# A looped prefix-logsumexp kernel rebuilt in fp32: row sums inside partitions, two small matmuls, one broadcast join, four load and two store buffers

## The chip, the cores and the metric

The kernel runs on 1 core of one Trainium2 chip. The metric is the device time of one execution in microseconds (us); lower is better. A ratio is the one from the runs of two kernels in the same rounds; it is not quite the ratio of the medians quoted beside it. "Span" is the time that the profiler sees from the first to the last instruction, about 2 us less than the device time. In the profiles, ACT is ScalarE, DVE is VectorE, PE is TensorE (PEld its weight loads), POOL is GpSimd and SP is SyncE; PSUM is the memory into which the matmuls of these kernels write.

## The reference

```python
B, S, D = 8, 4096, 2048            # x: fp32, standard normal
out[:, 0] = x[:, 0]
for t in range(1, S):              # running log(sum(exp(x))) along S
    mx = maximum(out[:, t-1], x[:, t])
    out[:, t] = mx + log(exp(out[:, t-1] - mx) + exp(x[:, t] - mx))
```

So the output is log(cumsum(exp(x))) along S. It reads 268.4 MB and writes 268.4 MB.

## The kernel before

The input is cut into 64 tiles, 8 for each of the 8 batches. A tile is 128 partitions x 4 rows x 2048 columns in fp32, 4.19 MB, and is contiguous in memory: a partition holds four consecutive rows of S. Each tile goes through Exp (ACT), sums (PE and DVE) and Ln (ACT) in four column pieces of 512, in place, in one of five buffers.

```python
R, FD, NC, NB = 4, 512, 4, 5
io = [pool.tile([P, R, D], f32) for i in range(NB)]       # loaded, worked on and stored in place
et = [pool.tile([P, R, FD], bf16) for c in range(NC)]     # Exp of a piece
ps = [psum.tile([P, FD], f32) for c in range(NC)]

# SP: a load waits until its buffer has been stored
take(sp, stored[n], 16);  sp.dma_start(out=io[n][:], in_=x_v[...]).then_inc(loaded[n], 16)

# ACT, for each piece of a tile
act.activation(et[c][:], t[:, :, cols(c)], ACT.Exp)
act.activation(t[:, :, cols(c)], t[:, :, cols(c)], ACT.Ln)
# ... and one store of a whole tile: act.dma_start(out=dst, in_=io[n][:])

# PE, for each piece: 4 bf16 matmuls to the first rows' sums, 4 more to carry the piece's total on
for r in range(R): pe.matmul(ps[c][:], (Li if r == 0 else Ls)[:], et[c][:, r, :], ...)
for r in range(R): pe.matmul(ps[c][:], (Us if r == 0 else Ui)[:], et[c][:, r, :], ...)

# DVE, for each piece: one copy from PSUM and three adds of 512
dve.tensor_add(t[:, 1, sl], ps[c][:], et[c][:, 1, :])
dve.tensor_copy(t[:, 0, sl], ps[c][:])
dve.tensor_add(t[:, 2, sl], t[:, 1, sl], et[c][:, 2, :])
dve.tensor_add(t[:, 3, sl], t[:, 2, sl], et[c][:, 3, :])
# [cut: semaphores, loop bounds, the last tile's smaller stores]
```

The four masks Li, Ls, Ui and Us are built ahead of the block that holds the first load.

The softmax here doesn't subtract the row's maximum and nothing guards it: scores larger than these inputs give would overflow.

Of the kernel before, what the change touches and what calls it, by code (L numbers as in the profile page):

```python
# [9 lines left out]
def kernel(  # L10
# [19 lines left out]

    nc = tc.nc
    f32 = mybir.dt.float32
    bf16 = mybir.dt.bfloat16
# [9 lines left out]
    NC = D // FD  # L43
    NB = 5
    assert NC == 4 and NBLK >= 3

    const = ctx.enter_context(tc.tile_pool(name="const", bufs=1))
    Li = const.tile([P, P], bf16)
    masks.make_upper_triangular(nc, Li, val=1.0, diag=True)
    Ls = const.tile([P, P], bf16)  # L50
    masks.make_upper_triangular(nc, Ls, val=1.0, diag=False)
    Ui = const.tile([P, P], bf16)
    masks.make_lower_triangular(nc, Ui, val=1.0, diag=True)
    Us = const.tile([P, P], bf16)
    masks.make_lower_triangular(nc, Us, val=1.0, diag=False)
# [3 lines left out]
    io = [pool.tile([P, R, D], f32, name=f"io{i}", tag=f"io{i}") for i in range(NB)]  # L59
    et = [pool.tile([P, R, FD], bf16, name=f"et{c}", tag=f"et{c}") for c in range(NC)]  # L60
    ps = [psum.tile([P, FD], f32, name=f"ps{c}", tag=f"ps{c}") for c in range(NC)]

# [3 lines left out]
    def cols(c):  # L66
        return slice(c * FD, (c + 1) * FD)

    def take(engine, sem, n):

        engine.add_instruction(mybir.InstEventSemaphore(  # L71
            name=f"I-{nc.next_id()}", engine=engine.engine, ins=[], outs=[],
            sync_info=mybir.SyncInfo(
                on_wait=[mybir.SyncWait(
                    sync_type="semaphore", id=sem.num, ant_name=sem.name,
                    wait_mode="sem-ge-imm", wait_value=n,
                )],
                on_update=[mybir.SyncUpdate(
                    sync_type="semaphore", id=sem.num, ant_name=sem.name,
                    update_mode="sem-sub-imm", update_value=n,  # L80
                )],
            ),
        ))

    with tc.tile_critical():
        sem = lambda name: nc.alloc_semaphore(name)
        logs = sem("logs")
        parts = {c: sem(f"part{c}") for c in range(2, NC)}

        loaded = [sem(f"loaded{n}") for n in range(NB)]  # L90
        stored = [sem(f"stored{n}") for n in range(NB)]
        exps = [sem("exps0"), sem("exps1")]
        prefix = [sem("prefix0"), sem("prefix1")]
        copied = [sem("copied0"), sem("copied1")]
        added = [sem("added0"), sem("added1")]
        chain = [sem("chain0"), sem("chain1")]
        freed = [sem("freed0"), sem("freed1")]

        with nc.Block() as block:

            @block.sync
            def _(sp):
                def load(src, n):
                    sp.dma_start(out=io[n][:], in_=src).then_inc(loaded[n], 16)

                for i in range(NB):
                    load(x_v[i], i)
                turns = (NT - NB) // NB
                with sp.Fori(0, turns) as j:
                    for n in range(NB):  # L110
                        take(sp, stored[n], 16)
                        load(x_v[bass.ds(j * NB + (NB + n), 1)][0], n)
                for i in range(NB + turns * NB, NT):
                    take(sp, stored[i % NB], 16)
                    load(x_v[i], i % NB)
                for i in range(NT - NB, NT):

                    take(sp, stored[i % NB], 48 if i == NT - 1 else 16)

            @block.scalar  # L120
            def _(act):
                def exp(n, c):
                    t = io[n]
                    if c == 0:
                        take(act, loaded[n], 16)
                    act.activation(  # L126
                        et[c][:], t[:, :, cols(c)], ACT.Exp
                    )._wait_ge(freed[c % 2], c // 2 + 1).then_inc(exps[c % 2], 1)
                    if c >= 2:
                        take(act, freed[c % 2], 2)  # L130

                def ln(t, c, told=logs):
                    act.activation(  # L133
                        t[:, :, cols(c)], t[:, :, cols(c)], ACT.Ln
                    )._wait_ge(added[c % 2], c // 2 + 1).then_inc(told, 1)
                    if c >= 2:
                        take(act, added[c % 2], 2)

                def store(dst, n):
                    take(act, logs, NC)  # L140
                    act.dma_start(out=dst, in_=io[n][:]).then_inc(stored[n], 16)

                def turn(n, dst_above):
                    exp(n, 0)
                    if dst_above is not None:
                        ln(io[(n - 1) % NB], 2)
                    exp(n, 1)
                    if dst_above is not None:
                        ln(io[(n - 1) % NB], 3)
                        store(dst_above, (n - 1) % NB)  # L150
                    exp(n, 2)
                    ln(io[n], 0)
                    exp(n, 3)
                    ln(io[n], 1)

                turn(0, None)
                turns = (NT - 1) // NB
                with act.Fori(0, turns) as j:
                    for n in range(1, NB + 1):
                        turn(n % NB, o_v[bass.ds(j * NB + (n - 1), 1)][0])  # L160
                for i in range(1 + turns * NB, NT):
                    turn(i % NB, o_v[i - 1])
                last = stored[(NT - 1) % NB]
                t = io[(NT - 1) % NB]
                take(act, logs, 2)
                act.dma_start(
                    out=o_v[NT - 1][:, :, 0:2 * FD], in_=t[:, :, 0:2 * FD]
                ).then_inc(last, 16)
                for c in range(2, NC):
                    ln(t, c, parts[c])  # L170
                    take(act, parts[c], 1)
                    act.dma_start(  # L172
                        out=o_v[NT - 1][:, :, cols(c)], in_=t[:, :, cols(c)]
                    ).then_inc(last, 16)
                take(act, freed[0], 2)
                take(act, freed[1], 2)

            @block.tensor
            def _(pe):
                def front(c, first):  # L180
                    for r in range(R):
                        m = pe.matmul(  # L182
                            ps[c][:], (Li if r == 0 else Ls)[:], et[c][:, r, :],
                            start=first and r == 0, stop=r == R - 1, skip_group_check=True,
                        )
                        if r == 0:
                            m._wait_ge(exps[c % 2], c // 2 + 1)
                    m.then_inc(prefix[c % 2], 1)
                    if c >= 2:
                        take(pe, exps[c % 2], 2)  # L190

                def total(c, final):

                    if final:
                        pe.wait_ge(copied[c % 2], [1, 2, 2, 1][c]).then_inc(freed[c % 2], 1)
                    else:
                        for r in range(R):
                            m = pe.matmul(  # L198
                                ps[c][:], (Us if r == 0 else Ui)[:], et[c][:, r, :],
                                start=False, stop=r == R - 1, skip_group_check=True,  # L200
                            )
                            if r == 0:
                                m._wait_ge(copied[c % 2], [1, 2, 2, 1][c])
                        m.then_inc(freed[c % 2], 1)
                    if c in (1, 2):
                        take(pe, copied[c % 2], 2)

                def turn(first, final):
                    for c in range(NC):
                        front(c, first)  # L210
                        total((c - 1) % NC, first if c == 0 else final)


                pe.sem_inc(freed[0], 2)
                pe.sem_inc(freed[1], 1)
                with pe.Fori(0, B):
                    turn(True, False)
                    with pe.Fori(0, NBLK - 2):
                        turn(False, False)
                    turn(False, True)  # L220
                pe.wait_ge(copied[1], 1).then_inc(freed[1], 1)
# [60 lines left out]
```

## Time and profile before

| | before |
|---|---|
| device time, median | 1258.5 us (1257.97 to 1258.94, 4 runs) |
| span of the profiled run | 1256.5 us |
| busy: ACT, DVE, PE | 75%, 53%, 48% |
| DMA traffic, rate in the middle of the run | 536.9 MB, 433 GB/s |

First the page of the kernel before: busy time of each engine, then two rows of the 40 slices of the span (31.4 us each), namely the busy share of the DMA engines in tenths and what they moved.

```profile
## 1 busy us (share of the span) xinstructions
PE 605.2 (48%) x1872; PEld 196.9 (16%) x1920; DVE 659.9 (53%) x1024; ACT 936.7 (75%) x513; POOL 1.9 (0%) x12
...
DMA  8999999999999999999999999999999999999996
GB/s 377 423 433 432 433 433 433 433 432 434 432 431 432 434 434 433 434 433 434 433 434 434 434 433 432 434 434 433 432 433 433 434 431 434 432 432 431 434 434 275
```

No engine is near full, and the DMA row is 9 in all but the first and the last slice. This is the reading that everything else rests on: a tile is loaded and stored once, 8.39 MB, and at 433 GB/s that takes 19.4 us; 64 tiles take 1240 us of the 1256.5. The Trainium skill, "DMA: Bandwidth & Descriptors" (section "Issuing engines are not separate DMA queues"), says that DMAs of all issuing engines run on the same 16 DMA engines; the trace agrees: the queue of the loads and the queue of the stores each take 49.6% of those engines' time.

The groups of ACT in the kernel before; the columns are line, engine, operation, shapes and count, then busy us and mean ns of one, then idle time just ahead of them and who ended it:

```profile
L126 ACT ACTIVATE et<-io 128x2048 bf16<-128x2048 f32 x256 | 486.5, 1901 | 302.1 <-ACTq L71 283.6
L133 ACT ACTIVATE io<-io 128x2048 f32<-128x2048 f32 x256 | 484.8, 1894 | 2.5 <-DVE io L236 1.7
```

ACT idles ahead of Exp, and its own queue ends that idle time. ACTq L71 is the helper through which ACT waits for a semaphore, here mostly "the load has landed".

Last the ends of the run. In the stretches view of the kernel before, each line is one stretch of time: its length, busy us of PE, PEld, DVE, ACT and POOL (with instructions), the granted PE clock, the DMA share and GB/s.

```profile
0.00:40.00 40.00, 14.85 (x51) 5.00 (x52) 16.87 (x27) 24.33 (x14) 1.87 (x12) 0.97 0.92 380
40.00:80.00 40.00, 24.85 (x86) 8.63 (x88) 27.06 (x43) 38.39 (x22) 0.00 (x0) 0.86 1.00 432
80.00:1176.00 1096.00, 536.27 (x1648) 173.94 (x1688) 581.75 (x903) 823.94 (x452) 0.00 (x0) 0.79 1.00 433
1176.00:1200.00 24.00, 11.14 (x39) 3.84 (x40) 13.61 (x22) 17.02 (x10) 0.00 (x0) 0.86 1.00 431
1200.00:1230.00 30.00, 15.17 (x43) 4.75 (x44) 13.68 (x22) 22.39 (x13) 0.00 (x0) 0.77 0.85 366
1230.00:1256.00 26.00, 2.92 (x8) 0.74 (x8) 6.95 (x11) 10.66 (x6) 0.00 (x0) 0.55 0.80 325
```

Over 1096 us in the middle the DMA share is 1.00 at 433 GB/s. All that is not DMA at full rate lies in the first 40 and the last 56 us.

### The profile page before, as it was taken

Reading aid. Unit: us, or ns where it says so; the run is one execution under the profiler, and the core shown is the slowest. Engines: PE = TensorE matmul, PEld = TensorE weight load, DVE = VectorE, ACT = ScalarE, POOL = GpSimd, SP = SyncE. Lnnn points to the kernel's source line nnn. Section 1 sums busy time; section 2 is a strip of 40 time slices with the busy share of each in tenths; the row PEclk is TensorE's granted clock in tenths of the full one; section 3 lists DMA queues with packets and bytes.
Section 4 is the critical chain, followed back from the end, with each engine's and each line's share of the span. In section 5 each row is a group of like instructions: output and inputs, shape, how many; then the busy total and the mean of one; then the engine's idle time right before and its main releaser. Section 6 shows DMA issues by size and latency. Waiting matters only on the chain. (4 is left out here: it accounts for less than half of the span.)

```text
span 1256.5 us, 6996 instructions
## 1 busy us (share of the span) xinstructions
PE 605.2 (48%) x1872; PEld 196.9 (16%) x1920; DVE 659.9 (53%) x1024; ACT 936.7 (75%) x513; POOL 1.9 (0%) x12
## 2 busy tenths in 40 slices
PE   3555445454454444554445444455455444544542
PEld 1111111111111111111111111111111111111110
DVE  3656455464554544555546455464555544545443
ACT  5988778777787777877878778777787777877774
POOL 0000000000000000000000000000000000000000
PEclk9888687885888858878688786887857888578785
DMA  8999999999999999999999999999999999999996
GB/s 377 423 433 432 433 433 433 433 432 434 432 431 432 434 434 433 434 433 434 433 434 434 434 433 432 434 434 433 432 433 433 434 431 434 432 432 431 434 434 275
DMA packets 19875, 536.90 MB, mean 427 GB/s; under 512 B 2080, under 2 KB 2080, under 8 KB 3616
## 3 DMA queue, kind: packets, MB, share of 16 engines
q10 hardware_dynamic: 10656, 268.44, 49.6%
q1 hardware_dynamic: 9216, 268.44, 49.6%
q14 instruction: 3, 0.02, 0.0%
HBM read 268.44 MB, written 268.44 MB: 427 GB/s over the span
## 5 line engine op out<-in xcount | busy, mean ns | idle before, releaser
L126 ACT ACTIVATE et<-io 128x2048 bf16<-128x2048 f32 x256 | 486.5, 1901 | 302.1 <-ACTq L71 283.6
L133 ACT ACTIVATE io<-io 128x2048 f32<-128x2048 f32 x256 | 484.8, 1894 | 2.5 <-DVE io L236 1.7
L229 DVE TENSOR_TENSOR io<-ps,et 128x512 f32<-128x512 f32 x256 | 177.1, 692 | 570.9 <-PE ps L182 568.7
L182 PE MATMUL ps<-et,Li 128*128 128x512 bf16 x256 | 126.5, 494 | 628.6 <-ACT et L126 627.8
L182 PE MATMUL ps<-et,Ls 128*128 128x512 bf16 x768 | 280.9, 487 | 0.0
L198 PE MATMUL ps<-et,Ui 128*128 128x512 bf16 x624 | 213.0, 455 | 2.9 <-issue 0.4
L236 DVE TENSOR_TENSOR io<-io,et 128x512 f32<-128x512 f32 x256 | 177.1, 692 | 8.9
L233 DVE TENSOR_TENSOR io<-io,et 128x512 f32<-128x512 f32 x256 | 174.5, 681 | 0.0
L232 DVE COPY io<-ps 128x512 f32<-128x512 f32 x256 | 174.3, 681 | 0.0
L182 PEld LDWEIGHTS ps<-et,Li 128*128 128x128 bf16 x256 | 25.5, 100 | 787.4 <-ACT et L126 787.2
L182 PEld LDWEIGHTS ps<-et,Ls 128*128 128x128 bf16 x768 | 89.8, 117 | 98.1 <-issue 66.3
L198 PE MATMUL ps<-et,Us 128*128 128x512 bf16 x224 | 103.7, 463 | 0.3 <-DVE io L232 0.3
L198 PEld LDWEIGHTS ps<-et,Ui 128*128 128x128 bf16 x672 | 77.1, 115 | 113.4 <-issue 60.1
L198 PEld LDWEIGHTS ps<-et,Us 128*128 128x128 bf16 x224 | 26.1, 116 | 40.4 <-issue 22.7
L35 ACT ACT_TABLE_LOAD x1 | 1.3, 1283 | 0.8 <-PEq L266 0.8
masks.py:102 POOL TENSOR_SCALAR_AFFINE_SELECT Ui<-Ui 128x128 bf16<-128x128 bf16 x1 | 0.3, 296 | 0.0
masks.py:102 POOL TENSOR_SCALAR_AFFINE_SELECT Us<-Us 128x128 bf16<-128x128 bf16 x1 | 0.3, 295 | 0.0
masks.py:66 POOL TENSOR_SCALAR_AFFINE_SELECT Ls<-Ls 128x128 bf16<-128x128 bf16 x1 | 0.3, 294 | 0.0
masks.py:66 POOL TENSOR_SCALAR_AFFINE_SELECT Li<-Li 128x128 bf16<-128x128 bf16 x1 | 0.3, 293 | 0.0
masks.py:101 POOL MEMSET Ui<- 128x128 bf16 x1 | 0.2, 207 | 0.0
masks.py:101 POOL MEMSET Us<- 128x128 bf16 x1 | 0.2, 207 | 0.0
masks.py:65 POOL MEMSET Ls<- 128x128 bf16 x1 | 0.2, 206 | 0.0
(5 smaller groups left out, 0.6 us busy)
## 6 DMA issues: line engine op xcount, KB each, us to landing
io<-in_x_dram SPq DMA_DIRECT2D x64, 4096.0 KB, 31.5
out_dram<-io ACTq DMA_DIRECT2D x63, 4096.0 KB, 38.7
out_dram<-io ACTq DMA_DIRECT2D x1, 2048.0 KB, 11.1
out_dram<-io ACTq DMA_DIRECT2D x2, 1024.0 KB, 11.8
```

What stands on the lines that cost most here:

```text
L35: nc.scalar.preload_act_table_set("natural_log_exp_and_others")
L126: act.activation(et[c][:], t[:, :, cols(c)], ACT.Exp)._wait_ge(freed[c % 2], c // 2 + 1).then_inc(exps[c % 2], 1)
L133: act.activation(t[:, :, cols(c)], t[:, :, cols(c)], ACT.Ln)._wait_ge(added[c % 2], c // 2 + 1).then_inc(told, 1)
L182: m = pe.matmul(ps[c][:], (Li if r == 0 else Ls)[:], et[c][:, r, :], start=first and r == 0, stop=r == R - 1, skip_group_check=True,)
L198: m = pe.matmul(ps[c][:], (Us if r == 0 else Ui)[:], et[c][:, r, :], start=False, stop=r == R - 1, skip_group_check=True,)
L229: dve.tensor_add(t[:, 1, sl], ps[c][:], et[c][:, 1, :])._wait_ge(prefix[q], c // 2 + 1).then_inc(chain[q], 1)
L232: dve.tensor_copy(t[:, 0, sl], ps[c][:]).then_inc(copied[q], 1)
L233: dve.tensor_add(t[:, 2, sl], t[:, 1, sl], et[c][:, 2, :])._wait_ge(chain[q], base + 1).then_inc(chain[q], 1)
L236: dve.tensor_add(t[:, 3, sl], t[:, 2, sl], et[c][:, 3, :])._wait_ge(chain[q], base + 2).then_inc(added[q], 1)
```

## The change

The new kernel does the sums in fp32 and mostly on DVE. In each partition, three adds turn the four rows into running sums. One fp32 "triangle" matmul on the last row gives each partition the sum of all partitions ahead of it; one "carry" matmul with a mask that selects the last partition brings the total of all earlier tiles into the next tile's PSUM. One add then joins that PSUM row, broadcast over the four rows, to the tile. All steps work on half tiles of 1024 columns. Inputs have four buffers, freed by Ln and no longer by the store; outputs have two of their own. The masks are built by POOL beside the first loads.

```diff
-    NB = 5
+    NI, NO = 4, 2
+    HALF = D // 2
-    # [cut: four bf16 masks, built ahead of the block]
+    before = pool.tile([P, P], f32); last = pool.tile([P, P], f32)
-    io = [... for i in range(NB)]; et = [...bf16...]; ps = [psum.tile([P, FD], f32) ... 4]
+    ti = [pool.tile([P, R, D], f32) for i in range(NI)]
+    to = [pool.tile([P, R, D], f32) for i in range(NO)]
+    ps = [psum.tile([P, D], f32) for i in range(2)]
 # SP
-    take(sp, stored[n], 16); load(...)
+    sp.wait_ge(freed, n + 1); load(...)
 # ACT, a turn
-    exp 0, ln 2 (tile above), exp 1, ln 3 (tile above), store, exp 2, ln 0, exp 3, ln 1
+    exp(n, 0); exp(n, 1)
+    ln(n - 1, 0); ln(n - 1, 1)        # ln(.., 0) first takes stored[n % NO]
+    done(n - 1)                       # frees the input buffer
+    store(n - 1)
 # PE
-    8 bf16 matmuls for each of 4 pieces
+    triangle(k, h): 2 fp32 matmuls  ps[k % 2]       += before^T @ ti[k][:, 3, half h]
+    carry(k, h):    2 fp32 matmuls  ps[(k + 1) % 2]  = last^T   @ ti[k][:, 3, half h]
 # DVE
-    for each of 4 pieces: add, copy, add, add of 512
+    local(n, h): for r in 1..3: t[:, r, half] += t[:, r - 1, half]        # 3 adds of 1024
+    join(n, h):  t[:, :, half] += ps[n % 2][:, half] broadcast over r     # 1 add of 4096
```

(Semaphore bookkeeping and the last tiles' smaller stores are left out. In the last turn alone, Ln of tile 62's first half and its store stand ahead of Exp of tile 63.)

## The prediction

> **What bounds it now.** The DMA. The page's slices show the 16 DMA engines 90% busy or more and 431 to 434 GB/s in 36 of 40 slices; the DMA queue table gives 536.9 MB, half loads, half stores. 536.9 MB at 433.5 GB/s is 1238.5 us of the 1256.5 us span. The other 18 us are the ends: the stretch table shows the first 5 us at 105 GB/s, the 10 us stretches from 1216 us on at 383, 275, 403 and 184 GB/s. Per 4.19 MB tile that is 19.4 us of DMA, for load and store. ACT is busy 75% (14.6 us a tile), DVE 53%, PE 48%. The waits view agrees: Exp waits 284 us for its load (named ACTq), matmuls wait 627 us for Exp.
>
> **What the change does.** Same bytes, same 4 MB transfers. So it can only win at the ends, and lose if something else needs more than 19.4 us a tile.
>
> - ACT: 8 instructions of 2048 elements (1.80 us start to start) become 4 of 4096, about 3.5 us each: 14.2 us a tile. Slightly less.
> - DVE: 16 instructions of 0.60 to 0.71 us spacing (10.3 us a tile) become 6 dependent adds of 1024 and 2 joins of 4096 elements. The Trainium skill, "VectorE: DVE Perf Modes" (the TRN2 errata section), gives an fp32 add as (N+151)/0.96 ns; the trace agrees at 512 (692 ns). Estimate: 1.24 and 4.42 us, so 16.3 us a tile; DVE becomes the busiest engine, near 83 to 85%.
> - PE: about 29 bf16 matmuls a tile become 8 in fp32 (4 in a batch's last tile). "FP8 and Floating Point Precision" (TensorE Precision Notes) says true fp32 takes 4 passes; no trace here shows it yet. From the 0.42 us spacing at the low clock: 1.7 us each, 3.4 us a half, 14 us a tile cold, half of that warm.
> - The loop through DVE, by hand: local h0, local h1 (7.5 us), with triangle h0 behind local h1; join h0 with triangle h1 behind it; join h1 with carry h0; carry h1 under the next tile's local h0. Everything on PE hides if a half's two matmuls take under about 3.75 us; the loop is then 16.5 to 17 us. It reaches 19.4 us only if they take about 5 us.
> - Buffers: an input buffer is now held about 27 us from Exp's start to Ln's end rather than through the store, so 4 leave over 40 us for a load within 77 us. Two store buffers allow a store about 31 us; sharing DMA evenly with a load it needs 20 to 22. A load is always queued, so DMA should stay saturated.
> - Ends: loads no longer wait for four masks (about 1.8 us saved). The tail is coarser: half-tile Exp, adds, join, Ln, and 2 MB last stores; Exp of the last tile to the last store's landing about 33 us against about 32 before. Short moments with loads alone (419 GB/s in the stretch table) may cost some us.
>
> **Prediction: 1259 us, 1250 to 1273.** Faster by over 2%: 1%. Within 2%: 92%. Slower by over 2%: 7%.
>
> **Signs.** Right: DMA 9 in nearly all slices at about 433 GB/s; DVE near 84%, ACT near 73%; joins 4.4 us; fp32 matmuls 0.9 to 1.8 us; Exp or Ln waiting for DMA, not for PE. Wrong: DMA below 9 in the middle, Ln waiting for PE, DVE waiting for the triangle.
>
> **What would make it wrong.** Fp32 matmuls (with their weight loads) over 2.5 us; joins slowed by the PSUM broadcast to over 5.5 us; two store buffers making Ln wait so long that all load buffers fill and the queues run dry; a tail where tiles queue behind the 16.5 us loop without loads to fill DMA.

## The result, and the profile after

| | before | after |
|---|---|---|
| device time, median | 1258.5 us | 1259.14 us (1258.89 to 1259.56, 4 runs) |
| ratio | | 1.0006, 95% interval 0.9988 to 1.0023 |
| span | 1256.5 us | 1257.2 us |
| busy: ACT, DVE, PE | 75%, 53%, 48% | 73%, 81%, 52% |
| instructions | 6996 | 3678 |

The page of the changed kernel, the same rows as above:

```profile
PE 651.9 (52%) x960; PEld 215.2 (17%) x960; DVE 1023.2 (81%) x512; ACT 913.3 (73%) x257; POOL 1.1 (0%) x8
...
DMA  9999999999999999999999999999999999999997
GB/s 400 407 434 433 434 434 432 434 434 434 434 432 433 433 433 434 433 433 433 434 434 432 433 434 434 434 433 433 434 432 434 434 434 434 433 434 433 433 399 285
```

DVE's work rose by more than half, from 659.9 to 1023.2 us, and the middle of the GB/s row did not move. The groups of ACT, DVE and PE, from the same page:

```profile
L132 ACT ACTIVATE to<-ti 128x4096 f32<-128x4096 f32 x128 | 456.3, 3609 | 267.0 <-ACTq L61 258.5
L232 DVE TENSOR_TENSOR ti<-ti 128x1024 f32<-128x1024 f32 x384 | 464.7, 1224 | 211.3 <-ACT ti L127 202.6
L241 DVE TENSOR_TENSOR ti<-ti,ps 128x4096 f32<-128x4096 f32 x128 | 560.0, 4417 | 9.7 <-PE ps L208 9.0
L208 PE MATMUL ps<-ti,before 128*128 128x512 f32 x512 | 383.0, 900 | 352.6 <-DVE ti L232 352.2
L127 ACT ACTIVATE ti<-ti 128x4096 f32<-128x4096 f32 x128 | 455.9, 3609 | 66.9 <-ACTq L61 66.9
```

Read the third column. The joins (L241) wait 9 us in the whole run for PE, so PE hides. DVE's adds (L232) wait 203 us for Exp: DVE has time left. And Ln (L132) waits 258 us on a semaphore of ACT's queue, while Exp (L127) waits only 67. In the kernel before it was Exp that waited. Which semaphore Ln waits for shows in the time line of one tile in the changed kernel (start, length, what; the idle time ahead of it in brackets; PE's weight loads are left out):

```profile
616.91 0.35 ACTq L140 DMA_DIRECT2D out_dram<-to  x1
617.40 7.12 ACT L127 ACTIVATE ti<-ti 128x4096 f32<-128x4096 f32 x2 [0.72 <-ACTq L61]
621.05 7.40 DVE L232 TENSOR_TENSOR ti<-ti 128x1024 f32<-128x1024 f32 x6 [3.06 <-ACT ti L127]
624.85 3.42 PE L208 MATMUL ps<-ti,before 128*128 128x512 f32 x4 [13.00 <-DVE ti L232]
628.36 8.74 DVE L241 TENSOR_TENSOR ti<-ti,ps 128x4096 f32<-128x4096 f32 x2
628.50 1.98 PE L208 MATMUL ps<-ti,before 128*128 128x512 f32 x4 [0.24 <-DVE ti L232]
629.00 7.12 ACT L132 ACTIVATE to<-ti 128x4096 f32<-128x4096 f32 x2 [4.48 <-ACTq L61]
636.36 0.35 ACTq L140 DMA_DIRECT2D out_dram<-to  x1
```

Exp starts as soon as the store before it is issued (0.72 us, ACT's own issue). Then ACT is idle for 4.48 us ahead of the first of the two Ln. The signal from PE that this Ln also waits for follows the joins of its own tile, and these had ended at 617.98 us (609.23 + 8.75; the tile is the last of its batch and has no carry). What is left is the store buffer. The two stores of this window lie 19.45 us apart, which is the DMA's time for one tile. The landing times, from the parts "DMA issues" of the two pages, say the same. Before:

```profile
io<-in_x_dram SPq DMA_DIRECT2D x64, 4096.0 KB, 31.5
out_dram<-io ACTq DMA_DIRECT2D x63, 4096.0 KB, 38.7
```

After:

```profile
ti<-in_x_dram SPq DMA_DIRECT2D x64, 4096.0 KB, 28.8
out_dram<-to ACTq DMA_DIRECT2D x62, 4096.0 KB, 31.4
```

The last number is the median us from issue to landing. A store now lands in 31.4 us; with the 7.4 us of Ln and its issue that makes 38.8 us, two periods of 19.4, for two buffers. The store takes just as long as the loop allows it to.

The stretches of the changed kernel, beside which those of before can be laid:

```profile
0.00:40.00 40.00, 13.67 (x20) 4.53 (x20) 22.75 (x14) 22.77 (x7) 1.09 (x8) 0.92 0.96 406
40.00:80.00 40.00, 22.65 (x41) 7.29 (x40) 39.51 (x19) 35.23 (x10) 0.00 (x0) 0.93 0.99 413
80.00:1176.00 1096.00, 583.67 (x852) 192.98 (x852) 906.89 (x456) 800.64 (x226) 0.00 (x0) 0.77 1.00 433
1176.00:1200.00 24.00, 12.70 (x19) 4.59 (x20) 20.18 (x10) 18.80 (x6) 0.00 (x0) 0.81 1.00 433
1200.00:1230.00 30.00, 13.52 (x22) 3.90 (x20) 19.92 (x11) 23.76 (x8) 0.00 (x0) 0.78 0.89 381
1230.00:1256.00 26.00, 5.64 (x8) 1.85 (x8) 13.98 (x7) 12.15 (x4) 0.00 (x0) 0.63 0.73 290
```

The middle is equal: share 1.00, 433 GB/s. The ends can be turned into time by (difference in GB/s) x (length) / 433. In the first 40 us the change gains 2.4 us (406 against 380; the first load goes out at 1.03 us and not at 2.82). In the next 40 it loses 1.8 us: the first store is issued at 40.07 us against 34.72, when the four first loads have nearly drained (read from the trace, not tested by itself). From 1200 to 1230 it gains 1.0 us, and in the last 26 us it loses 2.1. The sum is a loss of about half a microsecond; the spans differ by 0.7.

### The profile page after: what moved, and what is told of

It reads as the page before. It is cut to its first block, busy times and chain, and to the rows that moved or that the text cites. A ratio compares the mean times of both kernels' runs of the same rounds, so it can differ in the third digit from the quotient of the medians. Undisturbed runs are those within 1.5% of the kernel's fastest.

```text
span 1257.2 us, 3678 instructions
## 1 busy us (share of the span) xinstructions
PE 651.9 (52%) x960; PEld 215.2 (17%) x960; DVE 1023.2 (81%) x512; ACT 913.3 (73%) x257; POOL 1.1 (0%) x8
## 5 line engine op out<-in xcount | busy, mean ns | idle before, releaser
L132 ACT ACTIVATE to<-ti 128x4096 f32<-128x4096 f32 x128 | 456.3, 3609 | 267.0 <-ACTq L61 258.5
L232 DVE TENSOR_TENSOR ti<-ti 128x1024 f32<-128x1024 f32 x384 | 464.7, 1224 | 211.3 <-ACT ti L127 202.6
L241 DVE TENSOR_TENSOR ti<-ti,ps 128x4096 f32<-128x4096 f32 x128 | 560.0, 4417 | 9.7 <-PE ps L208 9.0
L208 PE MATMUL ps<-ti,before 128*128 128x512 f32 x512 | 383.0, 900 | 352.6 <-DVE ti L232 352.2
L127 ACT ACTIVATE ti<-ti 128x4096 f32<-128x4096 f32 x128 | 455.9, 3609 | 66.9 <-ACTq L61 66.9
L197 PE MATMUL ps<-ti,last 128*128 128x512 f32 x448 | 268.9, 731 | 232.9 <-DVE ti L241 232.9
L208 PEld LDWEIGHTS ps<-ti,before 128*128 128x128 f32 x512 | 129.7, 281 | 621.4 <-DVE ti L232 513.4
L197 PEld LDWEIGHTS ps<-ti,last 128*128 128x128 f32 x448 | 85.4, 211 | 399.9 <-DVE ti L241 334.8
## 6 DMA issues: line engine op xcount, KB each, us to landing
ti<-in_x_dram SPq DMA_DIRECT2D x64, 4096.0 KB, 28.8
out_dram<-to ACTq DMA_DIRECT2D x62, 4096.0 KB, 31.4
```

The source lines that it names most:

```text
L127: act.activation(t[:, :, half(h)], t[:, :, half(h)], ACT.Exp).then_inc(exps[h], 1)
L132: act.activation(to[n % NO][:, :, half(h)], ti[n % NI][:, :, half(h)], ACT.Ln)._wait_ge(carried[h], turn + 1).then_inc(logs, 1)
L197: m = pe.matmul(ps[(k + 1) % 2][:, sl], last[:], ti[k % NI][:, R - 1, sl], start=True, stop=False, skip_group_check=True,)
L208: m = pe.matmul(ps[k % 2][:, sl], before[:], ti[k % NI][:, R - 1, sl], start=k == 0, stop=True, skip_group_check=True,)
L232: a = dve.tensor_add(t[:, r, half(h)], t[:, r - 1, half(h)], t[:, r, half(h)])
L241: dve.tensor_add(t[:, :, half(h)], t[:, :, half(h)], ps[n % 2][:, half(h)].unsqueeze(1).to_broadcast([P, R, HALF]),)._wait_ge(ahead[h], n ...
```

## The experiments

The theory: the DMA engines set the time of both kernels, at 19.4 us a tile; the new engine work fits under it; only the ends can differ. Rivals: (1) the changed kernel is paced by its own loop on the engines, and its 19.4 us a tile is a coincidence; (2) it is paced by the latency of its two store buffers, for which Ln visibly waits; (3) it lies on the edge, so that any added work would show. Each run below was taken in the same rounds and on the same chip as the kernel before, not always on one chip with its neighbours here. The changed kernel itself was not run again, so a difference to its 1259.14 us is one across chips; the median of the kernel before was 1258.27 to 1258.5 us on all of them.

### copy_only: the transfers without the compute

```diff
-    Exp, sums, Ln in between
+    act.wait_ge(loaded[i % 5], ...)
+    act.dma_start(out=o_v[i], in_=io[i % 5][:])     # 64 loads, 64 stores, nothing else
```

> Wrong result on purpose: only the same 64 loads and 64 stores of 4 MB, no compute, five buffers. If the DMA engines set the time of both kernels, 536.9 MB at about 433 GB/s is 1238.5 us, and with the start and the last landing 1243 to 1250 us. If the loop through the engines or through the two store buffers sets the 19.4 us a tile, the bare copy should be clearly faster, under 1200 us.

Measured: 1247.44 us (2 runs; wrong result), the kernel before 1258.36 on that chip. In the stretches view of this run, where the one engine listed is POOL:

```profile
80.00:1176.00 1096.00, 0.00 (x0) 1.00 1.00 433
```

With no compute at all the middle also moves 433 GB/s. Rivals 1 and 2 cannot be what sets that rate. All that either kernel could still win with these transfers is the 11 to 12 us between it and this copy, and these lie at the ends.

### a_quarter_store and b_quarter_store: what the DMA hides

```diff
-    act.dma_start(out=dst, in_=t)
+    act.dma_start(out=dst[:, 0:1, :], in_=t[:, 0:1, :])      # a quarter of the bytes, in both kernels
```

> The changed kernel with stores of a quarter of the bytes (wrong result on purpose); the DMA work falls from 19.4 to about 12.1 us a tile. If DMA bounds the changed kernel, it now falls to its loop through DVE, 16.4 to 17 us a tile: 1085 to 1130 us. If its compute is what takes 19.4 us a tile, it stays near 1255 us.

> The kernel before with stores of a quarter of the bytes (wrong result on purpose). If DMA bounds it, it falls to ACT's 14.6 us a tile: 960 to 1010 us, well below the changed kernel with the same cut, which would show the DVE work that the change adds and that the full stores hide. If it is bound by something else, it stays near 1255 us.

Measured: the changed kernel 1061.65 us, the kernel before 993.03 us (2 runs each, wrong results). Both fall once the DMA has less to do, so both were bound by their transfers; smaller stores also free the store buffers sooner (in 15.0 us), so this run alone does not tell the DMA's rate from rival 2. Below the DMA they are not equal: the changed kernel is 68.6 us slower, about 1.1 us a tile. This is the cost of the change that the full stores hide.

The expectation for the kernel before, 960 to 1010 us, held; that for the changed kernel, 1085 to 1130 us, missed by a little. Its time line shows the true length of the loop:

```profile
611.62 7.39 DVE L232 TENSOR_TENSOR ti<-ti 128x1024 f32<-128x1024 f32 x6
...
618.93 8.74 DVE L241 TENSOR_TENSOR ti<-ti,ps 128x4096 f32<-128x4096 f32 x2
...
627.59 7.39 DVE L232 TENSOR_TENSOR ti<-ti 128x1024 f32<-128x1024 f32 x6
```

From one tile's adds to the next tile's adds it takes 627.59 - 611.62 = 15.97 us, with DVE never idle in this tile, and not the predicted 16.5 to 17. The slack under the DMA is 19.4 - 16.0 = 3.4 us a tile.

### a_dve_plus4 and a_dve_plus2: filling the slack

```diff
+                def extra(i):                            # 1024 elements, into a tile that nobody reads
+                    m = last[:].unsqueeze(1).to_broadcast([P, 8, P])
+                    dve.tensor_add(spare[:], m, m)._wait_ge(spent, i).then_inc(spent, 1)
                         for h in range(2):
                             local(n, h)
+                            extra(...)                   # once: two a tile; twice: four a tile
                         # [cut: the spare tile, its semaphore, one wait for the masks]
```

> The changed kernel with four more adds of 1024 elements a tile on DVE, 4.9 us. If the hidden loop takes about 16.4 us, it is now about 21.3 us a tile and past the DMA's 19.4: 1390 to 1430 us, with DMA no longer full. If DVE has more slack than the loop says, it stays at 1259 us; if DVE were already the bound, it would rise by all 4.9 us a tile to 1570 us.

> The changed kernel with two more adds of 1024 elements a tile on DVE, 2.45 us, so the loop is about 18.8 us, still under the DMA's 19.4. If DMA bounds it: 1259 to 1266 us, the few us from the first and last tiles alone, DVE busy over 90%. If DVE's loop is the bound: plus 157 us, 1415 us.

Measured: four extra adds 1368.18 us (2 runs, ratio 1.087 to the kernel before), with joins 20.75 us apart in its time line (817.84 and 838.59); two extra adds 1263.43 us (4 runs, ratio 1.0038, interval 1.0022 to 1.0055). Both results are correct. With two, the middle is untouched although DVE is now 92% busy in the whole run; the stretch of that run:

```profile
80.00:1176.00 1096.00, 626.07 (x860) 195.65 (x860) 1038.11 (x573) 807.80 (x227) 0.00 (x0) 0.73 1.00 433
```

The 157 us of added DVE work cost about 4 us over the changed kernel, at the ends. With four, the loop passes 19.4 us, the time follows it, and the DMA is no longer at its rate:

```profile
80.00:1280.00 1200.00, 656.54 (x870) 211.22 (x869) 1188.12 (x696) 829.08 (x232) 0.00 (x0) 0.71 0.98 404
```

The expected 1390 to 1430 us was too high because it started from the 16.4 us loop; (20.75 - 15.97) / 4 gives 1.195 us for each added add. Rivals 1 and 3 fall: 2.4 us of added work a tile (two adds) cost nothing in the middle, 4.8 us (four adds) cost time; the edge at 3.4 us lies between.

### a_carry_x2: twice the carry work on PE

```diff
-                    for c in range(2 * h, 2 * h + 2):
+                    for c in [2 * h, 2 * h + 1] * 2:     # the second pair overwrites the first
```

> The changed kernel with each carry matmul done twice (same result, the second overwrites). At the warm clock a half's carry is then about 4 us and still hides: 1259 to 1265 us. At the cold clock it is 6.8 us, the loop 21.5 us, and the time near 1400 us. Between these it shows how often the clock is low. If PE were on the critical path already, it would rise in any case.

Measured: 1260.29 us (2 runs, correct, ratio 1.0012, interval 0.9992 to 1.0032), PE busy 61% in place of 52%. The stretch of that run:

```profile
80.00:1176.00 1096.00, 689.32 (x1250) 250.49 (x1248) 904.78 (x456) 802.66 (x226) 0.00 (x0) 0.86 1.00 433
```

The granted clock was 0.86 there against 0.77. PE has room. What a carry of twice the length would do at the low clock stays open, since the added work came with a higher clock.

### a_one_store_buf: one store buffer in place of two

```diff
-    NI, NO = 4, 2
+    NI, NO = 4, 1      # [cut: the last tiles' waits count both half stores]
```

> The changed kernel with one store buffer in place of two. Ln then waits for the whole store of the tile before: 7.4 us of Ln plus a store that shares DMA with the load for part of its time, about 14 us: 21.5 us a tile, 1330 to 1480 us, DMA no longer full. If two store buffers are already what paces the changed kernel by latency and not by the DMA's rate, one should double the tile to about 39 us, 2400 us.

Measured: 1915.46 us (2 runs, correct), ratio 1.52. Neither number was right: 30 us a tile, where the theory had 21.5 and rival 2 had 39. The time line of this run shows why:

```profile
815.43 7.12 ACT L132 ACTIVATE to<-ti 128x4096 f32<-128x4096 f32 x2 [15.13 <-ACTq L61]
822.77 30.35 SPq L111 DMA_DIRECT2D ti<-in_x_dram  x2
822.80 0.35 ACTq L140 DMA_DIRECT2D out_dram<-to  x1
...
845.45 7.12 ACT L132 ACTIVATE to<-ti 128x4096 f32<-128x4096 f32 x2 [15.05 <-ACTq L61]
```

The end of Ln frees an input buffer and an output buffer at once, so the next load and the store are issued within 0.03 us of each other and share the DMA from start to end: the store's median landing is 22.6 us. I had let the load run in Ln's 7 us. So the shortest loop here is 7.4 + 22.6 = 30.0 us, and that is what was measured. For two buffers the same terms give an estimate of (7.4 + 22.6) / 2 = 15.0 us a tile, which is under 19.4. The run a_dve_plus4 bears it out with two buffers: its stores land in 24.1 us (median), and its list of waits, which has 258 us of Ln on ACT's queue in the changed kernel, has none there; Ln waits for PE instead, 344 us. Rival 2 is therefore not the bound with two buffers; it is one with one buffer. Ln's 4.5 us waits in the changed kernel are the place where ACT feels the full DMA, not the cause of the 19.4 us.

### b_early_loads: one part of the change alone

```diff
-    masks.make_upper_triangular(...) and three more, ahead of the block
+            @block.gpsimd                      # the same masks beside the first loads
+            def _(g): ...  g.affine_select(...).then_inc(shaped, 1)
+                pe.wait_ge(shaped, 4)
```

> The kernel before with one part of the change alone: the masks built beside the loads and not ahead of them, so the first load goes out at about 1.0 us instead of 2.8. If each us that the DMA starts earlier counts in full: 1256.5 to 1257 us, 1.8 us less. Then the changed kernel, which also has this, loses about 2.4 us elsewhere, at its ends.

Measured: 1256.54 us (5 runs, correct), the kernel before 1258.42 on that chip; ratio 0.9984, interval 0.9971 to 0.9998. The 1.9 us is the predicted 1.8. The changed kernel has this gain too and is not faster, so it loses about as much at its other ends.

### a_tail_order: the usual order in the last turn

```diff
                     final = n == NT - 1
-                    if final:
-                        ln(n - 1, 0, turn)
-                        act.wait_ge(logs, 2 * turn + 1)
-                        store(n - 1, o_v[n - 1], 0)
                     exp(n, 0)
                     exp(n, 1)
-                    if not final:
-                        ln(n - 1, 0, turn)
+                    ln(n - 1, 0, turn)
+                    if final:
+                        act.wait_ge(logs, 2 * turn + 1)
+                        store(n - 1, o_v[n - 1], 0)
```

> The changed kernel with Exp of the last tile ahead of Ln of the tile before it, as in all other turns; same work. If only the ends are left to win, the last tile's chain starts about 6 us earlier and the middle is unchanged at 433 GB/s: 1251 to 1255 us, against 1259. If the order at the end does not matter because the stores already queue, it stays at 1259 us.

Measured: 1254.47 us (1253.6 to 1256.88, 5 runs, correct), the kernel before 1258.42; ratio 0.9972, interval 0.9958 to 0.9985. This is the lowest median of the versions that compute the right result, 0.3% under the kernel before (the interval of a_ends below overlaps with this one). In the changed kernel the last tile's Exp starts at 1224.28 us and its last store is issued at 1248.05; here they stand at 1218.22 and 1241.77:

```profile
1218.22 7.12 ACT L127 ACTIVATE ti<-ti 128x4096 f32<-128x4096 f32 x2 [0.52 <-ACTq L61]
...
1241.77 0.54 ACTq L140 DMA_DIRECT2D out_dram<-to  x1
```

The last chain starts 6 us sooner, but the span shrinks by only 4.4 us (1257.2 to 1252.8): the last four stores are now issued 4.2 to 4.3 us apart, and the last one takes 9.6 us to land, not 7.7.

### a_half_stores and copy_cols: stores by column halves

The changed kernel with the new order at the end, and with every store in two:

```diff
-                    act.dma_start(out=dst, in_=t).then_inc(stored[n % NO], landing)
+                    act.dma_start(out=dst[:, :, half(h)], in_=t[:, :, half(h)]
+                    ).then_inc(stored[n % NO][h], 16)           # after each Ln; Ln(h) waits for its own half
                     # [cut: the semaphores of the halves, the order at the end]
```

> The changed kernel with that same order at the end and each tile's store as two halves of 2 MB, each issued and its buffer half freed after its own Ln. If the two store buffers' loop paces the middle, the middle gains too, far more than at the ends: under 1230 us. If DMA paces it, the middle stays at 433 GB/s and the ends gain some us more than the order alone: 1246 to 1253 us; if pieces of 4 KB move slower, it loses that again.

Measured: 1289.21 us (1281.92 to 1293.49, 5 runs, correct), ratio 1.0225, interval 1.0203 to 1.0248: slower, and outside both numbers; only the proviso about 4 KB pieces came true. The five runs scatter by 0.9%, and the profile is of the slowest. Its stretch:

```profile
80.00:1176.00 1096.00, 554.58 (x820) 182.84 (x820) 875.48 (x440) 778.09 (x219) 0.00 (x0) 0.76 1.01 420
```

The DMA is as full as ever, but moves 420 GB/s and not 433. To see whether the waits of this kernel matter, the bare copy got the same stores:

```diff
-                    act.dma_start(out=o_v[i], in_=io[i % NB][:])
+                    for h in range(2): act.dma_start(out=o_v[i][:, :, sl], in_=io[i % NB][:, :, sl])
                     # [cut: the waits count both halves]
```

> Wrong result on purpose: the bare copy with each store as two of 2 MB, by column halves (runs of 4 KB), as in the run with half stores. If it is the shape of these stores that slows the DMA, with no engine and no Ln waiting, the copy rises from 1247 us by about the 3% that the half-store kernel lost in its middle: 1275 to 1295 us, DMA still full. If that kernel was slow for its waits or its order of issue, the copy stays at 1245 to 1252 us.

Measured: 1281.76 us (2 runs, wrong result) against 1247.44 for the plain copy on another chip; the kernel before took 1258.27 and 1258.36 on the two. Its stretch:

```profile
80.00:1176.00 1096.00, 0.00 (x0) 1.00 1.01 421
```

So it is the shape of the stores and no wait: a full DMA at a lower rate. Half a row is a run of 4 KB, where a whole tile's partition is one run of 32 KB. This change also doubles the number of stores, and no run here tells the length of a run from the number of DMAs.

### a_ends: half stores for the last four tiles only

```diff
-                    if final:
-                        act.wait_ge(logs, 2 * turn + 1); store(n - 1, o_v[n - 1], 0)
+                    act.wait_ge(logs, 2 * turn + 1); store(n - 1, o_v[n - 1], 0)     # tiles 60 to 62 as well
                     # [cut: the second half's store; the waits count both half stores]
```

> The changed kernel with the new order at the end, and half stores only for the last four tiles, so that the DMA gets work sooner there. If the end is limited by stores that come late: 1251 to 1253.5 us, 1 to 3 us under the order alone. If those are limited by the DMA's rate for half stores, no gain: 1254 to 1256 us.

Measured: 1255.35 us (1255.19 to 1258.28, 5 runs, correct), ratio 0.9978, interval 0.9964 to 0.9991, against 0.9972 for the order alone. No gain over the order alone; the lower DMA rate of half stores may have eaten it, but that was not measured by itself.

## Why the prediction was right, and where it was not

The time was predicted as 1259 us and came out at 1259.14.

- **"The DMA bounds it", "it can only win at the ends": right.** The bare copy at 1247.44 us, with the same 433 GB/s in the middle, and the fall of both kernels with smaller stores show it.
- **ACT, "slightly less": right.** 14.2 us a tile predicted; 913.3 us over 64 tiles is 14.3.
- **DVE's instructions: right.** The Trainium skill, "VectorE: DVE Perf Modes" (section on the TRN2 errata), gives (N+151)/0.96 ns: 1224 and 4424; the trace has 1224 and 4417, and DVE is busy 81% against "83 to 85%". **The loop was mis-sized by a small term:** "16.5 to 17 us" was 15.97. The joins start 4.33 us apart and not 4.42, and the margin over the sum of 16.3 us was not needed.
- **PE: right.** "4 passes" (the Trainium skill, "FP8 and Floating Point Precision", TensorE Precision Notes) gave 3.4 us a half at the low clock; the time line has 3.42 there and 1.98 at the high clock. The joins waited for PE 9 us in the whole run.
- **Buffers: the step that failed.** "Two store buffers allow a store about 31 us; sharing DMA evenly with a load it needs 20 to 22" leaves the store time to spare. For a store that shares with one load the size was about right (22.6 us with one store buffer). In the changed kernel there was nothing to spare: stores took the whole 31.4 us, and it was Ln that waited for them. A load and a store are issued every 19.4 us, so 28.8 / 19.4 = 1.5 loads and 31.4 / 19.4 = 1.6 stores are under way at a time, on average, and not one of each. "A load is always queued" held: 28.8 us is longer than the time between two loads. The conclusion held too: with two buffers the loop could run at about 15 us a tile, so the DMA stays the bound.
- **Ends.** "About 1.8 us saved" by early loads was 1.9 in its own run. "Exp of the last tile to the last store's landing about 33 us against about 32" was 31.5 (1224.28 to 1248.05, plus 7.7 to land) against 33.1 (1221.73 to 1242.29, plus 12.6): the same size, with the sign turned. The cost sat elsewhere: the last tile's Exp started 2.6 us later than before, and the first store 5.3 us later. The prediction had sized neither. That it met the time within 0.2 us is luck: these small terms cancel.

## What to carry to other kernels

When a time line shows the DMA full from end to end, first measure the bare copy with the same transfers: it says how much any change to the compute can bring, here 11 us of 1258. A wait in front of an engine does not name the bound; compute the shortest loop through that buffer, and compare it with the period. Work hidden under a bound is not free: the change used up over 1 us a tile of slack that a later, lighter store would bring to light.

## What the Trainium skill lacked or had wrong

- "DMA: Bandwidth & Descriptors" (section "Where 436 GB/s comes from") has a sentence that for transfers between HBM and SBUF the HBM side, about 358 GB/s, binds. With one core running, 433 GB/s was held over 1096 us by loads and stores together, close to the 435 which the page has for the fabric. The page's own measured rates, which it marks as single-core, reach 425 GB/s; the sentence lacks that mark. "HBM Reference" has it right in saying that a core alone measures well above its share.
- The same page's specifications put the transfer size for line rate at 512 B or more. Stores by column halves, 4 KB runs, moved 420 and 421 GB/s with a full DMA where whole tiles moved 433. No page compares runs of 4 KB with longer ones on this chip. These stores are also twice as many, and no run tells the two apart, so the row is not shown to be wrong.
- "FP8 and Floating Point Precision" gives four passes for true fp32, and two fp32 matmuls took 3.42 us at the low clock, four times the 0.43 us of a bf16 one, each. No page says how that looks in a trace: each fp32 matmul is two MATMUL records and two weight loads (960 records for 480 matmuls).
- "VectorE: DVE Perf Modes" has the length of an fp32 add right (1224 ns at 1024 elements), but its remark that a next instruction which is not held starts earlier has no time for it: joins of 4417 ns started 4.33 us apart, and an added add of 1221 ns cost 1.195 us in the loop.
